# Hybrid backbone, one core: direct products in one block, Fourier products among value tiles, smaller angle tables given later

## The chip, the cores and the metric

The kernel runs on one core of one Trainium2 chip. The metric is the device time of one execution in microseconds (us), the median over runs. The core has a matrix engine (PE), a vector engine (DVE), an activation engine (ACT), a general engine (POOL), and SyncE (SP), whose instruction queue issues the DMA transfers spoken of here. Each engine works through its own list of instructions in order, and semaphores hold an instruction back until what it needs is there.

## What is computed

Two layers over 2048 latent tokens (a grid 64 wide) and 256 context tokens, 1024 channels. Layer 0 has a Fourier mixer (256 channels) beside a neighbourhood attention (12 heads of 64), layer 1 a gated MLP beside a bidirectional S5 scan. Cut to what matters here:

```python
def even_mixer(hl, hc, w_in, w_out, rpb, with_ctx_out):
    fa_l, ga_l, q_l, k_l, v_l, gb_l = split_cols(hl @ w_in, EVEN_SPLITS)
    ...
    a_l = fourier_mix(fa_l) * jax.nn.silu(ga_l)
    n_l = neighbourhood_attention(heads(q_l), heads(k_l), heads(v_l), k_c, v_c, rpb) * jax.nn.silu(gb_l)
    y_l = jnp.concatenate([a_l, n_l], axis=-1) @ w_out

def fourier_mix(v):
    y = jnp.fft.fftn(vg, axes=(1, 3), norm="ortho").real   # vg: (B, L, groups, 64)

def s5_direction(u_lat, u_ctx, lam_re, lam_im, log_step, b_re, b_im, c_re, c_im, reverse, with_ctx_out):
    lam_bar, b_bar = s5_discretise(lam_re, lam_im, log_step, b_re, b_im)
    ...
    h_lat = linear_scan(lam_bar, drive(u_lat), h_end, reverse)
    return read(h_lat), ...
```

The tables of the S5 scan depend on the weights alone: powers of `lam_bar` ("turn" tables), products of those with `B` and `C`, and a 16-step convolution kernel worked out from them ("direct products").

## The kernel before

All of what the change touches lies in the first fifth of the kernel, in `run()`. Weights in float32 are split into two float16 parts: the load fills a staging buffer `wf` (L154, a ring of four), DVE takes the maximum per partition (L156), PE and DVE take it across partitions (L109, L111) and to a power of two (L92 to L100), ACT writes the high part `wh` (L189) and DVE the low part `wl` (L190). A product is then three groups of eight matmuls of 256 or 512 columns (L181), and its result is split again in the same way (ACT L189, DVE L190).

`run()` calls, one after another: `s5_prep` (with `v_proj` of the first and second block of 256 value channels handed in as work to lie between), `v_proj(2)` for the third block, `fourier_first`, and `need((0, 5))`, which starts `heads`, the queries, keys and gates of the first pair of heads and the attention's first loads. The written order is not the order on the engines: each call gives its instructions in a stream ("", "b", "f") with PSUM banks of its own, and a scheduler then merges the streams by its own estimate of times, for each engine. Where a tile's memory is used again, the new owner waits for the old one.

- `v_proj(blk)`: 18 tiles of 128 tokens by 256 channels, each 24 matmuls on PE, one eviction on ACT, one on DVE, two stores.
- `s5_prep`: complex products (`cmul`, L1109 to L1114) on DVE and POOL, tables `W` written to DRAM (`mo_d`), then, after `v_proj(1)`, in pool "s5pk": eight groups `q` of direct products. Each loads a tile `ws` (576 KB, L1314) and a tile `bs` (64 KB, L1315) from DRAM, two buffers each, multiplies them in 32 small matmuls (L1319), copies four strips out on ACT (L1328), adds `db` on DVE (L1329) and stores `kp_d` (L1330).
- At the end of the same pool: eight angle tables. Each is a complex product of the two turn tables, six DVE instructions of 1152 columns (L1109 to L1114 by way of `cmul`), into a tile `rot` that is stored in `rot_d` (1152 KB). They are read again only in the S5 scan of layer 1 (`E`).
- `fourier_first`: 16 products of a table `d1` with a strip `Z` of the Fourier input, both loaded (L559, L561, three buffers each), 4 matmuls each on PE (L564), copied on ACT (L566) and stored (L567); then two context products (L573, L577).
- `heads` for pair 0 begins with three weight loads and splits, and then runs on PE (L181).

## Time and profile before

| what | us |
|---|---|
| median of three runs | 2430.7 (2428.79 to 2432.24) |
| the profiled execution, its own time | 2425.14 |
| its span (first to last instruction) | 2423.3 |
| PE busy in the span | 2219.7 |
| DVE busy | 1579.7 |
| ACT busy | 1050.9 |
| POOL busy | 336.3 |

One execution was profiled; the 1.8 us beside the span lie around the program. "Busy" leaves out register, branch and DMA-issuing instructions. In rows of a timeline the columns are start, duration, engine, line, operation, output and inputs with their shape, how many like it were merged, and in brackets the idle time ahead and who ended it. `PEclk` is the granted clock of PE as a share of full speed.

### The profile page before, as it was taken

To read this page: it belongs to the slowest core of one execution; us is meant where nothing else is said; L and a number is where in the kernel's file an instruction comes from. 1 tells how busy PE (TensorE), PEld (TensorE's weight loads), DVE (VectorE), ACT (ScalarE), POOL (GpSimd) and SP (SyncE) were. 2 spreads that over 40 slices of the span, in tenths; PEclk is the share of its full clock that TensorE was granted. 3 is DMA by queue.
4 is the path that set the end of the run, shared out by engine and by line. 5 is a ranking of instruction groups with operands and counts; after the bars stand their busy time and mean duration, and the time that the engine had idled before them with its cause. 6 is when DMAs were issued, how large, how long until landed. Compare 5 with 4: busy or idle time off the path is not lost. (4 is left out here: it accounts for less than half of the span.)

```text
span 2423.3 us, 42852 instructions
## 1 busy us (share of the span) xinstructions
PE 2219.7 (92%) x15860; PEld 1421.6 (59%) x15860; DVE 1579.7 (65%) x3949; ACT 1050.9 (43%) x2212; POOL 336.3 (14%) x457
## 2 busy tenths in 40 slices
PE   5999885999999999999978899997899999999998
PEld 2668773476665767666657466556555565444443
DVE  5888892266567666666569667774496952458455
ACT  4822222155555656565557454552221221334332
POOL 0102200022222322222234000000010011110000
PEclk8999998999999999999998899998899999999999
DMA  9844677413335243433342444545466751256332
GB/s 320 264 108 127 168 236 231 131 54 95 115 103 149 81 119 106 116 114 93 96 167 86 137 140 135 158 134 164 143 182 195 200 152 48 80 156 194 122 113 87
DMA packets 349971, 340.57 MB, mean 141 GB/s; under 512 B 94482, under 2 KB 291486, under 8 KB 347970
## 3 DMA queue, kind: packets, MB, share of 16 engines
q1 hardware_dynamic: 349650, 337.80, 46.5%
q8 instruction: 125, 2.05, 0.4%
q14 instruction: 84, 0.69, 0.1%
q10 hardware_dynamic: 112, 0.03, 0.0%
HBM read 218.43 MB, written 110.91 MB: 136 GB/s over the span
## 5 line engine op out<-in xcount | busy, mean ns | idle before, releaser
L181 PEld LDWEIGHTS <-wh 128*128 128x128 f16 x2944 | 281.8, 99 | 169.0 <-issue 9.2
L1000 DVE CUSTOM_DVE_ANT_0 P<-S,bias,slab 128x640 f32<-128x640 f32 (+2 forms) x216 | 193.6, 896 | 161.0 <-PE S L997 157.0
L189 ACT ACTIVATE ph<-PT 128x384 f16<-128x384 f32 (+1 forms) x408 | 172.6, 456 | 216.4 <-PE PT L1016 215.6
L181 PEld LDWEIGHTS <-wl 128*128 128x128 f16 x1472 | 144.0, 100 | 112.0 <-issue 27.4
L190 DVE SCALAR_TENSOR_TENSOR pl<-PT,ph 128x384 f16<-128x384 f32 (+1 forms) x408 | 195.0, 508 | 13.8 <-ACT ph L189 12.4
L949 POOL TENSOR_TENSOR bias<-G,masks 128x384 f32<-128x384 f32 (+1 forms) x144 | 152.3, 1058 | 345.5 <-DVE t L1000 322.5
L1002 ACT ACTIVATE P<-P,t 128x640 f32<-128x640 f32 (+2 forms) x216 | 181.2, 839 | 41.4 <-DVE t L1000 40.0
L181 PE MATMUL pg<-hh,wl 128*128 128x512 f16 (+1 forms) x800 | 184.6, 365 | 13.7 <-DVE stg L190 5.6
L181 PEld LDWEIGHTS <-h1p 128*128 128x128 f16 x1152 | 111.1, 98 | 136.6 <-issue 8.8
L181 PE MATMUL pu<-wh,h1p 128*128 128x512 f16 x768 | 179.9, 379 | 1.6 <-DMA h1p<-h 1.6
L181 PE MATMUL pg<-hl,wh 128*128 128x512 f16 (+1 forms) x800 | 181.2, 360 | 0.0
L181 PE MATMUL pg<-hh,wh 128*128 128x512 f16 (+1 forms) x800 | 181.2, 359 | 0.0
L181 PEld LDWEIGHTS <-yh 128*128 128x128 f16 x1088 | 106.8, 98 | 125.4 <-issue 2.7
L1016 PE MATMUL PT<-ident,P 128*128 128x128 f32 x1104 | 162.3, 277 | 11.3 <-DVE pl L190 9.8
L997 PEld LDWEIGHTS <-Q 128*128 128x128 f16 x1776 | 131.6, 98 | 63.1 <-issue 22.7
L997 PE MATMUL S<-K,Q 128*128 128x128 f16 (+1 forms) x1776 | 158.4, 233 | 2.4 <-DVE t L1000 2.2
L181 PE MATMUL pg<-wh,yl 128*128 128x512 f16 x544 | 133.3, 386 | 5.2 <-DVE yl L190 5.1
L1016 PEld LDWEIGHTS PT<-ident,P 128*128 128x128 f32 x1104 | 120.3, 142 | 20.2 <-issue 6.8
L181 PE MATMUL pg<-wl,yh 128*128 128x512 f16 x544 | 131.3, 382 | 0.0
L156 DVE TENSOR_REDUCE t<-wf 128x1 f32<-128x1024 f32 x68 | 82.4, 1216 | 74.8 <-DMA wf<-in_w_in_even_dram 27.0
L181 PE MATMUL pg<-wh,yh 128*128 128x512 f16 x544 | 130.3, 379 | 0.0
L181 PEld LDWEIGHTS <-hh 128*128 128x128 f16 x1152 | 115.5, 100 | 15.7
(344 smaller groups left out, 3952.6 us busy)
## 6 DMA issues: line engine op xcount, KB each, us to landing
wada<-in_w_ada_dram SPq DMA_DIRECT2D x34, 512.0 KB
x<-in_x_dram SPq DMA_DIRECT2D x32, 512.0 KB
wf<-in_w_in_even_dram SPq DMA_DIRECT2D x28, 512.0 KB
V<-vs SPq DMA_DIRECT2D x192, 64.0 KB
K<-kd SPq DMA_DIRECT2D x96, 128.0 KB
wf<-in_w_in_odd_dram SPq DMA_DIRECT2D x20, 512.0 KB
rot_d<-rot SPq DMA_DIRECT2D x8, 1152.0 KB
Y<-ys SPq DMA_DIRECT2D x144, 64.0 KB
```

Source lines behind the costliest of these rows:

```text
L156: nc.vector.tensor_reduce(m[:, i:i + 1], f, axis=AX.X, op=OP.max, apply_absolute_value=True)
L181: nc.tensor.matmul(ps, a(k), b(k), start=(n == 0), stop=(n == 3 * kb - 1))
L189: nc.scalar.activation(hi, src, AF.Copy, scale=scale)
L190: nc.vector.scalar_tensor_tensor(lo, src, scale, hi, op0=OP.mult, op1=OP.subtract)
L949: nc.gpsimd.tensor_tensor(q4(bv), gv, q4(masks[:, m0:m0 + 128 * nch]), op=OP.add)
L997: nc.tensor.matmul(S[:, at:at + m], u["q"], K[:, hl, off:off + m], start=(hl == 1), stop=(hl == 0))
L1000: nc.vector.tensor_tensor_reduce(P[:, 0:n], S[:, 0:n], u["B"][:, 0:n], u["negf"], 3.4e38, OP.add, OP.min, nm)
L1002: nc.scalar.activation(P[:, 0:n], P[:, 0:n], AF.Exp, bias=nm, scale=-1.0, accum_out=l)
L1016: self.nc.tensor.transpose(PT[:, c - a:c - a + 128], P[:, c:c + 128], self.ident)
```

## The change

`s5_prep` keeps only the tables up to `v_proj(1)`. The direct products move to a function `s5_direct`, and their tiles `ws` and `bs` are halved: 16 loads of 288 KB and 16 of 32 KB in place of 8 and 8, still two buffers each. The angle tables move to `s5_angles`: 16 tables in place of 8, six DVE instructions of 576 columns each, one of the two products made in place in the table (`tq` is the only other tile, one buffer); `rot_d` has a new layout and `s5_states` reads it contiguously. The turn tables and the angle tiles lie in pools of their own, on the right side of memory.

Ahead of `v_proj(2)`, `heads` is started and stepped until its first pair's weights are loaded and split. `fourier_first` becomes a generator: its first four pairs of loads are given ahead of `v_proj(2)`, its products after it in stream "f", with four buffers for `d1` and `Z` and two for the copies. The angle tables are given after that.

```diff
@@ run() @@
-                    with self.stream("b"):
-                        self.s5_prep([lambda: self.v_proj(gp, 0), lambda: self.v_proj(gp, 1)])
-                    self.v_proj(gp, 2)
-                    qp = hTs.enter_context(self.pool_("qkg"))
-                    with self.pool_("fft") as fp, self.stream("f"):
-                        self.fourier_first(fp)
-                    self.gpool = hTs.enter_context(self.pool_("gates"))
-                    self.steps = self.mixed(self.heads(qp), self.ada_steps(), ADA_EVERY)
-                    self.ahead, self.credit, self.at, self.made = None, 0.0, (0, 0), -1
-                    self.need((0, 5))
+                    with self.pool_("s5r", side="right") as rp, self.pool_("s5e", side="right") as ep:
+                        with self.stream("b"):
+                            self.s5_prep(rp, [lambda: self.v_proj(gp, 0), lambda: self.v_proj(gp, 1)])
+                            self.s5_direct()
+                        qp = hTs.enter_context(self.pool_("qkg"))
+                        self.steps = self.mixed(self.heads(qp), self.ada_steps(), ADA_EVERY)
+                        self.ahead, self.credit, self.at, self.made = None, 0.0, (0, 0), -1
+                        while self.ahead is None:
+                            self.step()
+                        with self.pool_("fft") as fp:
+                            first = self.fourier_first(fp)
+                            next(first)
+                            self.v_proj(gp, 2)
+                            with self.stream("f"):
+                                for _ in first:
+                                    pass
+                        self.s5_angles(ep)
+                        self.gpool = hTs.enter_context(self.pool_("gates"))
+                        self.need((0, 5))
@@ s5_direct(), was in s5_prep() @@
             for q in range(8):
-                ws = pool.tile([128, 4, 2, 144], F32, name=self.name("ws"), tag="ws", bufs=2)
-                bs = pool.tile([128, 4, 2, 16], F32, name=self.name("bs"), tag="bs", bufs=2)
...
+                    if j == 0:
+                        g = 4 * q + j4
+                        ws = pool.tile([128, 2, 2, 144], F32, name=self.name("ws"), tag="ws", bufs=2)
+                        bs = pool.tile([128, 2, 2, 16], F32, name=self.name("bs"), tag="bs", bufs=2)
@@ s5_angles() @@
+        for i in range(16):
...
+            for r, op in ((0, OP.subtract), (1, OP.add)):
+                t = pool.tile([128, 2, 18, 16], F32, name=self.name("tq"), tag="tq", bufs=1)
+                nc.vector.tensor_tensor(v(e[:, r]), x[0], y[r], op=OP.mult)
+                nc.vector.tensor_tensor(t, x[1], y[1 - r], op=OP.mult)
+                nc.vector.tensor_tensor(v(e[:, r]), v(e[:, r]), t, op=op)
+            nc.sync.dma_start(self.rot_d[j, h, d], e.rearrange("p r g n -> p (r g n)"))
```

What the scheduler makes of it is seen in the lists of the engines; the lines of the changed kernel are some 20 further down (L1319 becomes L1346, L564 becomes L583, L1329 becomes L1356).

PE, before, where the second group of direct products ends (`ws_3674`, the second of eight) and the first tile of `v_proj(2)` begins (`pg_3980`, weights `wh_3973`):

```order
L1319 MATMUL pg_3678<-ws_3674,bs_3675 16x16 x2
L1319 MATMUL pg_3678<-ws_3674,bs_3675 16x112 x2
L1319 MATMUL pg_3678<-ws_3674,bs_3675 16x16 x2
L1319 MATMUL pg_3678<-ws_3674,bs_3675 16x112 x2
L1319 MATMUL pg_3678<-ws_3674,bs_3675 16x16 x2
L181 LDWEIGHTS hl_79
L181 MATMUL pg_3980<-wh_3973,hl_79 128x256
L181 LDWEIGHTS hl_79
L181 MATMUL pg_3980<-wh_3973,hl_79 128x256
```

PE, after, the same place (`ws_3898` is the last half of the last group, `mx_4026` the maximum over the weights of `v_proj(2)`, `Z` a Fourier strip, `wh_4038` the weights of `v_proj(2)`):

```order
L1346 MATMUL pg_3885<-ws_3898,bs_3899 16x112 x2
L1346 MATMUL pg_3885<-ws_3898,bs_3899 16x16 x2
L109 MATMUL mx_4026<-ident,t_4024 128x128
L583 MATMUL pg_4585<-Z_4003,d_639_4001 128x256 x2
L583 MATMUL pg_4595<-Z_4007,d_641_4005 128x256 x2
L583 MATMUL pg_4605<-Z_4011,d_643_4009 128x256 x2
L583 MATMUL pg_4615<-Z_4015,d_645_4013 128x256 x2
L583 MATMUL pg_4625<-Z_4590,d_695_4588 128x256 x2
L181 LDWEIGHTS hl_79
L181 MATMUL pg_4045<-wh_4038,hl_79 128x256
L181 LDWEIGHTS hl_79
```

Before, groups three to eight follow between tiles of `v_proj(2)`, and the 16 Fourier products stand in a row behind its last tile. Now all eight groups stand in one block with nothing of another stream between them; behind it come the maximum, five Fourier products and then `v_proj(2)`, whose tiles have the other eleven Fourier products between them.

DVE, before, among the complex products of `s5_prep`, at the start of `v_proj(1)` (`wl_3974` is the low part of the weights of `v_proj(2)`):

```order
L1112 TENSOR_TENSOR p_2718<-p_1862,p_1865 128x4x128
L1113 TENSOR_TENSOR p_2719<-p_1862,p_1864 128x4x128
L190 SCALAR_TENSOR_TENSOR wl_3974<-wf_3953,slab_217,wh_3973 128x1024
L1114 TENSOR_TENSOR p_2823<-p_2718,p_2719 128x512
L190 SCALAR_TENSOR_TENSOR wl_3974<-wf_3956,slab_217,wh_3973 128x1024
L190 SCALAR_TENSOR_TENSOR v_3115<-pg_3090,v_3115 128x4x64
```

DVE, after, behind the last adds of the direct products (`wl_3944`, `wl_3964`, `wl_3980` are the low parts of the first pair's weights, `wl_4039` that of `v_proj(2)`'s):

```order
L190 SCALAR_TENSOR_TENSOR wl_3964<-wf_3928,slab_217,wh_3963 128x1024
L190 SCALAR_TENSOR_TENSOR wl_3980<-wf_3948,slab_217,wh_3979 128x1024
L1373 TENSOR_TENSOR tq_4910<-turn_1858,turn_1857 128x576
L156 TENSOR_REDUCE t_4017<-wf_4021 128x1
L1374 TENSOR_TENSOR rot_4905<-rot_4905,tq_4910 128x576
L161 TENSOR_REDUCE t_4024<-t_4017 128x1
L156 TENSOR_REDUCE t_5160<-wf_5161 128x1
L156 TENSOR_REDUCE t_5224<-wf_5225 128x1
L111 TENSOR_REDUCE t_4028<-mx_4026 128x1
...
L190 SCALAR_TENSOR_TENSOR wl_4039<-wf_4018,slab_217,wh_4038 128x1024
L190 SCALAR_TENSOR_TENSOR wl_4039<-wf_4021,slab_217,wh_4038 128x1024
```

The weights of `v_proj(2)` are made 190 places later than before, behind the three splits of the first pair's weights. Of the angle tables' 96 instructions 58 stand between the turn tables and the last eviction of `v_proj(1)`, beside the same complex products and evictions as before; before there were 5 there.

SP, after, the end of the direct products' loads (`kp_d` and `rot_d` are stores; `wf_4021` is the second half of the weights of `v_proj(2)`, `wf_5161` and `wf_5225` belong to the second pair of heads):

```order
L1344 DMA bs_3887<-bst_d 128x4x16
L1343 DMA ws_3898<-mo_d 128x4x144
L1344 DMA bs_3899<-bst_d 128x4x16
L1357 DMA kp_d<-p_3636 128x240
L1375 DMA rot_d<-rot_4885 128x1152
L1357 DMA kp_d<-p_3637 128x240
L1375 DMA rot_d<-rot_4895 128x1152
L154 DMA wf_4021<-in_w_in_even_dram 128x4x256
L154 DMA wf_5161<-in_w_in_even_dram 128x8x128
L154 DMA wf_5225<-in_w_in_even_dram 128x8x128
```

Before, both halves of the weights of `v_proj(2)` are loaded ahead of the first value tiles. Now the second half comes behind the last store of `kp_d`, and takes the staging buffer that the first of the three splits gives back.

## Rows read from the trace of the kernel before

**Rows 1.** The page: busy time, and the chain that ended last.

```profile
PE 2219.7 (92%) x15860; PEld 1421.6 (59%) x15860; DVE 1579.7 (65%) x3949; ACT 1050.9 (43%) x2212; POOL 336.3 (14%) x457
...
PE 16%; DVE 1%; DMA 1%; issue 0%; ACT 0%; SPq 0%; ACTq 0%; DVEq 0%
```

**Rows 2.** Busy time by stretch: start and end, length, engines, clock, DMA.

```profile
188.20:292.60 104.40, 91.64 (x774) 79.17 (x771) 87.91 (x116) 26.27 (x65) 33.76 (x24) 0.93 0.54 145
292.60:357.60 65.00, 62.55 (x689) 55.65 (x688) 58.60 (x88) 18.14 (x50) 0.00 (x0) 1.00 0.77 235
357.60:415.40 57.80, 26.57 (x91) 17.20 (x90) 14.37 (x48) 13.87 (x22) 0.62 (x2) 0.84 0.65 223
```

**Rows 3.** Timeline of PE, Fourier stage and the start of heads.

```profile
373.98 6.63 PE L564 MATMUL pg<-Z,d 128*128 128x256 f32 x16 [16.27 <-DMA Z<-fa_d]
...
402.09 1.10 PE L564 MATMUL pg<-Z,d 128*128 128x256 f32 x4 [0.22 <-DMA Z<-fa_d]
403.02 1.88 PE L573 MATMUL pg<-dctx,zc 128*128 128x512 f32 x4
...
415.39 1.89 PE L181 MATMUL pg<-hh,wl 128*128 128x256 f16 x8 [3.94 <-DVE slab L717]
...
447.94 3.36 PE L181 MATMUL pg<-hh,wl 128*128 128x512 f16 x8 [3.76 <-DVE stg L190]
```

**Rows 4.** Matmuls of 292.6 to 415.4 by line and shape.

```profile
L564 PE MATMUL pg<-Z,d 128*128 128x256 f32 x64 | 19.7, 449 | 25.7 <-DMA Z<-fa_d 25.0 <-ACT a L566 0.8
L181 PE MATMUL pg<-wh,hh 128*128 128x256 f16 x145 | 19.3, 273 | 0.0
```

**Rows 5.** Timeline of PE, first direct products.

```profile
293.41 1.83 PE L1319 MATMUL pg<-ws,bs 128*16 128x112 f32 x32 [0.71 <-DMA bs<-bst_d]
295.81 1.83 PE L1319 MATMUL pg<-ws,bs 128*16 128x112 f32 x32 [0.57 <-DMA bs<-bst_d]
```

**Rows 6.** Timeline of DVE, products of 576 columns back to back.

```profile
237.94 0.74 DVE L1279 TENSOR_TENSOR p<-p,p 128x576 f32<-128x576 f32 x1
238.61 0.74 DVE L1278 TENSOR_TENSOR p<-p,p 128x576 f32<-128x576 f32 x1
```

**Rows 7.** DVE by line and shape, 188.2 to 292.6.

```profile
L190 DVE SCALAR_TENSOR_TENSOR v<-pg,v 128x256 f16<-128x256 f32 x29 | 12.0, 418 | 14.0 <-ACT v L189 13.8
...
L190 DVE SCALAR_TENSOR_TENSOR wl<-wf,slab,wh 128x1024 f16<-128x1024 f32 x2 | 3.4, 1696 | 0.0
L156 DVE TENSOR_REDUCE t<-wf 128x1 f32<-128x1024 f32 x2 | 2.3, 1200 | 0.0
...
L1110 DVE TENSOR_TENSOR p<-turn,turn 128x1152 f32<-128x1152 f32 x1 | 1.4, 1352 | 0.0
```

**Rows 8.** DMA issues of SP, first groups of direct products.

```profile
291.13 1.58 SPq L1315 DMA_DIRECT2D bs<-bst_d  x1
...
299.21 0.38 SPq L1314 DMA_DIRECT2D ws<-mo_d  x1
299.63 0.95 SPq L1315 DMA_DIRECT2D bs<-bst_d  x1
```

**Rows 9.** DMA issues of SP, last Fourier strip.

```profile
399.79 0.39 SPq L561 DMA_DIRECT2D Z<-fa_d  x1
```

**Rows 10.** ACT by line and shape, copies of the direct products.

```profile
L1328 ACT ACTIVATE p<-pg 16x240 f32<-16x240 f32 x32 | 11.5, 361 | 0.7
```

**Rows 11.** DMA issue of SP, a weight load.

```profile
417.72 0.38 SPq L154 DMA_DIRECT2D wf<-in_w_in_even_dram  x1
```

**Rows 12.** Timeline of DVE, maxima over loaded weights.

```profile
424.78 1.22 DVE L156 TENSOR_REDUCE t<-wf 128x1 f32<-128x1024 f32 x1 [0.99 <-DMA wf<-in_w_in_even_dram]
...
446.07 1.22 DVE L156 TENSOR_REDUCE t<-wf 128x1 f32<-128x1024 f32 x1 [10.89 <-DMA wf<-in_w_in_even_dram]
```

**Rows 13.** Timeline of PE, matmuls behind an idle stretch.

```profile
269.55 1.03 PE L181 MATMUL pg<-wh,hl 128*128 128x256 f16 x8 [2.86 <-DVE v L190]
...
271.86 1.92 PE L181 MATMUL pg<-wh,hh 128*128 128x256 f16 x8
```

More of the change, by code (lines that the diff above doesn't have):

```diff
@@ L556, in fourier_first, with load @@
         self.gg_d = self.dram.tile([2, 128, SEQ], F32, name="gg_d")
+        got = []
+        def load():
+            n2 = len(got)
+            dt = pool.tile([128, 2, 128], F32, name=self.name("d1"), tag="d1", bufs=4)
+            nc.sync.dma_start(dt, I["k_dft1"][:, n2])
+            Z = pool.tile([128, 256], F32, name=self.name("Z"), tag="Z", bufs=4)
+            nc.sync.dma_start(Z, dap(self.fa_d, n2 * 256, [[16 * 256, 128], [1, 256]]))
+            got.append((dt, Z))
+        for _ in range(4):
+            load()
+        yield
         for n2 in range(16):
-            dt = pool.tile([128, 2, 128], F32, name=self.name("d1"), tag="d1", bufs=3)
-            nc.sync.dma_start(dt, I["k_dft1"][:, n2])
-            Z = pool.tile([128, 256], F32, name=self.name("Z"), tag="Z", bufs=3)
-            nc.sync.dma_start(Z, dap(self.fa_d, n2 * 256, [[16 * 256, 128], [1, 256]]))
+            dt, Z = got[n2]
             ps = self.psg()
@@ L564, in fourier_first @@
                 nc.tensor.matmul(ps[:, cs * 256:(cs + 1) * 256], dt[:, cs, :], Z, start=True, stop=True)
-            a = pool.tile([128, 512], F32, name=self.name("a1"), tag="a1", bufs=3)
+            if n2 < 12:
+                load()
+            a = pool.tile([128, 512], F32, name=self.name("a1"), tag="a1", bufs=2)
             nc.scalar.activation(a, ps, AF.Copy)
@@ L1123, in s5_prep @@
         bst_d = self.dram.tile([32 * 4 * 64, 16], F32, name="bst_d")
-        self.rot_d = self.dram.tile([4, 2, 128, 2 * 4 * 288], F32, name="rot_d")
+        self.rot_d = self.dram.tile([4, 2, 2, 128, 2 * 2 * 288], F32, name="rot_d")
         self.mag8 = self.const.tile([128, 32], F32, name="mag8")
-        rots = ExitStack()
-        rp = rots.enter_context(self.pool_("s5r"))
-        turn = [rp.tile([128, 2, 32, n], F32, name=f"turn{n}") for n in (16, 18)]
+        self.turn_t = turn = [rp.tile([128, 2, 32, n], F32, name=f"turn{n}") for n in (16, 18)]
         with self.pool_("s5p") as pool, ExitStack() as early:
@@ L1330, in s5_prep, with s5_angles @@
                 self.bq.dma_start(self.kp_d[q], kp)
[L1332 to L1341 removed]
+    def s5_angles(self, pool):
+        nc = self.nc
+        turn = self.turn_t
+        v = lambda a: a.rearrange("p g (b k) -> p g b k", k=16)
+        for i in range(16):
+            j, h, d = i // 4, i // 2 % 2, i % 2
+            e = pool.tile([128, 2, 2, 288], F32, name=self.name("rot"), tag="rot", bufs=2)
+            q = slice(16 * d + 2 * (i // 2), 16 * d + 2 * (i // 2) + 2)
+            x = [turn[1][:, r, q, :, None].to_broadcast([128, 2, 18, 16]) for r in range(2)]
+            y = [turn[0][:, r, q, None, :].to_broadcast([128, 2, 18, 16]) for r in range(2)]
+            for r, op in ((0, OP.subtract), (1, OP.add)):
[4 more added lines that the diff above has]
+            nc.sync.dma_start(self.rot_d[j, h, d], e.rearrange("p r g n -> p (r g n)"))
     def out_proj(self, pool, lh, ll, w, u_y, ssq, sx, sq=None):
```

28 lines of the change are left out of this document (11 added, 17 removed).

## The prediction

> **What bounds the kernel now.** The page comes first. PE is busy 2219.7 of 2423.3 us and DVE 1579.7, and the chain that ended last is PE's where it names an engine [rows 1]. So the kernel is bound by PE, and what can be gained is about 200 us in which PE stands idle. The table by stretch then shows where that is for this change [rows 2]. Up to 292.6 (end of `v_proj(1)`) PE works 91.64 of 104.40 us, and DVE 87.91: DVE is nearly full here. From 292.6 to 357.6 (direct products among the tiles of `v_proj(2)`) PE works 62.55 of 65.00. From 357.6 to 415.4, the Fourier stage, PE works 26.57 of 57.80 at a granted clock of 0.84: 31 us of idle time, and slow matmuls besides. These 31 us are what there is to win. The timeline tells why: the first Fourier product waits 16.27 us for its strip `Z`, the products take until 403 us, two context products follow, and after 3.94 us more (the split of the first pair's weights) `heads` starts at 415.39 [rows 3]. By line, the Fourier products waited 25.0 us for `Z` and worked 19.7 [rows 4].
>
> **The change: what I compare.** All parts end before the start of `heads`, so I work out that moment, 415.4 before, and correct for what comes later. On PE, 122.8 us lie between 292.6 and 415.4. The PE work in them is: direct products 8 x 1.83 = 14.6 [rows 5]; `v_proj(2)`, 18 tiles of 24 matmuls (145 of one of their three kinds [rows 4]), about 48, which is what the direct products leave of the 62.55 [rows 2]; 16 Fourier products, 0.93 each from start to start (402.09 to 403.02), 15; two context products of two parts, the longer part 1.88 each, 6 in all [rows 3]. Together 84; some 39 us are holes and half clock. The change can save no more than these 39 here.
>
> **Angle tables moved up: `v_proj(1)` ends later.** The order has 58 angle instructions ahead of the last eviction of `v_proj(1)`, 5 before. One of 576 columns takes 0.67 us from start to start (237.94 to 238.61) [rows 6], so 58 are 38.9 us on DVE. Out of the stretch go 5 of 1152 columns at 1.35, and the two splits (3.4) and two maxima (2.3) of weights [rows 7], 12.4 in all. DVE's work is then 87.9 - 12.4 + 38.9 = 114.4 us, where the stretch is 104.4 long [rows 2]: DVE alone makes it 10 us longer. Its idle time of 16.5 us was almost wholly waiting for ACT's half of an eviction, 14.0 [rows 7], which is PE not being ready; with DVE late most of that goes. I keep 3.5 us of it: +13.5, with bounds of +7 (some tables slip behind, evictions are drained by the three `v` buffers) and +20 (half of the idle time stays). Before, 43 angle instructions ran beside the well-fed PE of `v_proj(2)`, and hid there; that cover is given up.
>
> **Direct products in a block: their loads come into the open.** Before, six of the eight groups lay between tiles of `v_proj(2)`, 47 us of PE work that covered every load. Now PE has nothing else from the first to the last. The loads come through two buffers of half a group. When a half is done its buffers are free; SP issues two loads (0.38 and up to 0.95 [rows 8]), they land, and PE multiplies 0.92. The landing: the second group's issue ended at 292.71 and its products started at 295.81, 3.1 us [rows 5, 8]; the last strip `Z`, issued at 399.79, was used at 402.09, 2.3 us [rows 3, 9]; counted from the start of the issue of `bs` it was 4.7. With 3.1, two halves take 0.1 + 0.9 + 3.1 + 0.9 = 5.0, and eight such rounds, less the two halves that are there at the start, 36 to 38 us. SP also has some 20 other DMAs in its row there (stores of `kp_d` and `rot_d`, the first Fourier loads, 0.4 each), and the stores wait for DVE; I take 41 us for the whole block. From below: the fastest that SP can issue 32 loads and 24 others, at 0.38 to 0.45 each, is 24, and the 10 MB that move in the block (5 of loads, 4 of tables, 1 of the rest) at the 235 GB/s of [rows 2] take 42, at twice that rate 21. So 24 to 50 by these rows, and 20 in a case that stands among the rivals, against 14.6 of plain work.
>
> The Trainium skill, "DMA: Bandwidth & Descriptors", section "Anatomy of one DMA — SWDGE (gpsimd) path", gives each DMA of that path a fixed cost of about 2.0 us that no size takes away, plus bytes / 436 GB/s. These loads are SP's, so it is a neighbour and no more; an estimate by it is 2.7 us for a half tile `ws` and 3.4 for a whole one: halving the tile saves a fifth of the landing and doubles their number, which speaks against this part of the change. By 2.7 the block would be 38 us and not 41.
>
> **The weights of `v_proj(2)` come last.** Before, they were split at the start of `v_proj(1)`, and nothing waited. Now their second half is behind the last store of `kp_d` in SP's list, and needs a staging buffer that only the first pair's first split frees. That split writes into memory which the direct products' pool held, so it waits for the last `kp_d` to land. From the last direct product to the first matmul of `v_proj(2)`: four copies of 0.36 [rows 10] and an add 1.7, store landing 3.1 as above, the split's two parts 2.8 (low part 1.7 at most [rows 7], high part as an estimate 1.1), the load of 512 KB (issued at 417.72, used at 424.78 [rows 11, 12]) 7.1, its maximum 1.2, the two other maxima that stand ahead in DVE's list 2.4 [rows 7], and from the maximum across partitions to split weights 3.9, as the first pair's took before [rows 3]: 22 us, bounds 18 (the load in 3.1) and 25. PE has five Fourier products in this time (about 7 us at the slow clock: four of them took 6.63 [rows 3]), which cost nothing. The clock falls behind such holes: after 2.86 us of waiting eight matmuls soon took 1.92 us where they had taken 1.03 [rows 13]; a few such groups at the start of `v_proj(2)`, 2 to 3 us, are inside the bounds.
>
> **What is won.** Behind it PE has `v_proj(2)` 48, eleven Fourier products at 0.93, 10.2, and context products 6: 64.2, and I take 64.5; the loads of `Z` are hidden by the tiles (four buffers, and two tiles of 2.6 us between products). The 31 us of idle time in the Fourier stage are gone, and so is the split of the first pair's weights (3.94 of it). `heads` starts at once.
>
> **The sum.** 292.6 + 13.5 + 41 + 22 + 64.5 = 433.6, or 18.2 us later than 415.4. After that, the order of all engines is as before but for the second pair's weights, which are now loaded early. Their maximum on DVE waited 10.89 us and held up an eviction, and PE stood 3.76 us and then ran eight matmuls in 3.36 instead of 1.89 [rows 3, 12]. That goes, 5.5 with the slow matmuls after it; what would be late next is the fourth weight load, which I leave at nothing, with a bound of 2 us. The new reading of the tables in layer 1 costs nothing: it is the same bytes, loaded ahead. So 18.2 - 5.5 = +12.7 us on the profiled execution's 2425.1: 2437.8. The median of the runs is 5.6 above that execution, so 2443 us as a median.
>
> **Rivals.**
> - *The loads keep up.* While PE works on one half the other lands: if SP issues at once and a half lands within some 1.3 us of that, the block is PE's 14.6 us and 16 waits of about 0.35, 20 us. The sum is then 21 less, `heads` starts at 412.6, and with the later 5.5 the kernel is 8.3 us faster: 2422. For it: the two waits that the trace shows for whole groups were 0.71 and 0.57 only [rows 5]. Against it: these were the first two groups, loaded into empty buffers, and every landing in the trace took 2.3 us or more. It decides below 23 us for the block.
> - *The pieces cancel.* A block of 34 us, angle tables at +9, 20 of chain: 419.6, 4.2 late, with the later gain 1 early: 2430.
> - *DVE is the wall.* If the idle time stays in `v_proj(1)` (+20), and the adds of the direct products stand behind 38 more angle instructions (25 us on DVE, in the same block) so that stores, copies and loads wait in turn and the block takes 50: 292.6 + 20 + 50 + 23 + 64.5 = 450, with the later gain 29 late: 2460. For it: DVE is at 84% before anything is added. Against it: in the block DVE has 25 us of work in 41.
> - *The change doesn't do what it says,* that is, the Fourier products don't fill anything: the order shows eleven of them between the tiles, so I give it nothing of its own; it would show as PE waiting for `Z` among the tiles.
>
> **How the numbers follow.** Forecast (+5 to +23 us) 0.50; loads keep up 0.14; pieces cancel 0.17; DVE is the wall 0.19. The time is that of the forecast, 2443. The range reaches from the lower side of "the pieces cancel", 2427, to 2460, and leaves out "loads keep up" and the worst of the last. About 0.2% is what a measurement of this kernel can tell from no change, 4.9 us: slower 0.69, within 0.17, faster 0.14.
>
> **What would show it right or wrong.** Right: `v_proj(1)` ends near 306; PE waits for `ws` or `bs` in most of the 16 halves and the block is about 40 long; some 20 us with only Fourier products; then tiles with no wait for `Z`; `heads` starts near 433 and there is no 3.8 us hole after its tenth eviction or so. Wrong: DVE idle in `v_proj(1)`, or products of one half straight behind the other, or the weights of `v_proj(2)` ready when the block ends (then 20 us of the sum are gone, and it is faster). The chain of 22 is the longest piece with no row of its own; if it is half, the result is even.

## The result: 0.5% slower, `heads` start 22.7 us late

The changed kernel takes 2439.23 us (median of 10 runs, 2435.32 to 2441.26) and the kernel before 2426.72 (10 runs on the same chip, 2420.06 to 2432.24): a ratio of 1.0051, 95% interval 1.0039 to 1.0062. That is 12.5 us slower; forecast were 12.7. The profiled execution of the changed kernel has a span of 2438.7 us, 15.4 more than that of before.

The page of the kernel after says little: PE (2218.4 us) and DVE (1582.6 us) are as busy as before, and the chain that ended last is PE's again [rows 1].

The table by stretch of the kernel after answers [rows 2]; I have put the borders where its own stages end: `v_proj(1)`, the block of direct products, the chain to the first tile of `v_proj(2)`, the tiles, and the start of `heads` (438.1). The columns are start and end, length, busy time of PE, PE's weight loads, DVE, ACT and POOL with counts, granted clock, DMA share, GB/s.

```profile
188.20:305.50 117.30, 93.96 (x793) 80.24 (x790) 115.19 (x166) 25.54 (x64) 35.51 (x24) 0.94 0.52 153
305.50:356.70 51.20, 25.71 (x257) 21.06 (x256) 28.55 (x66) 10.55 (x30) 0.00 (x0) 0.61 0.83 227
356.70:376.20 19.50, 7.29 (x22) 6.01 (x23) 16.45 (x29) 7.82 (x12) 0.00 (x0) 0.63 0.65 217
376.20:438.10 61.90, 61.14 (x489) 52.12 (x488) 11.70 (x23) 15.50 (x34) 0.00 (x0) 1.00 0.51 161
```

DVE is busy 115.2 of the first 117.3 us, and PE is busy 94.0 of them. In the second stretch PE is busy half the time at a granted clock of 0.61, and in the third, 19.5 us long, little more than a third. In the fourth PE is busy 61.1 of 61.9 at the full clock: there the change does what it is for. The timeline of PE, which answers [rows 3, 5]:

```profile
304.47 1.04 PE L181 MATMUL pg<-wh,hh 128*128 128x256 f16 x8
312.39 3.54 PE L1346 MATMUL pg<-ws,bs 128*16 128x112 f32 x32 [6.88 <-DMA bs<-bst_d]
...
336.26 3.16 PE L1346 MATMUL pg<-ws,bs 128*16 128x112 f32 x32 [2.44 <-DMA bs<-bst_d]
342.72 3.19 PE L1346 MATMUL pg<-ws,bs 128*16 128x112 f32 x32 [3.30 <-DMA bs<-bst_d]
348.00 3.27 PE L1346 MATMUL pg<-ws,bs 128*16 128x112 f32 x32 [2.09 <-DMA bs<-bst_d]
353.24 3.39 PE L1346 MATMUL pg<-ws,bs 128*16 128x112 f32 x32 [1.97 <-DMA bs<-bst_d]
368.91 0.79 PE L109 MATMUL mx<-ident,t 128*128 128x128 f32 x2 [12.28 <-DVE t L161]
369.50 6.89 PE L583 MATMUL pg<-Z,d 128*128 128x256 f32 x20
376.23 1.91 PE L181 MATMUL pg<-wh,hl 128*128 128x256 f16 x16
...
438.13 1.04 PE L181 MATMUL pg<-hh,wl 128*128 128x256 f16 x8
```

The last group of `v_proj(1)` starts at 304.47, the first direct product at 312.39, 6.88 us after PE fell idle. A row of 32 is two halves straight behind each other. The last of these pairs follow each other at 5.2 to 6.5 us (336.26, 342.72, 348.00, 353.24), and PE waits for `bs` ahead of each pair. From the end of the last product (356.63) PE waits 12.28 us for the maximum of the weights of `v_proj(2)`, does five Fourier products, starts `v_proj(2)` at 376.23 and `heads` at 438.13. The hole of 3.76 us that stood behind the 18th group of `heads` [rows 3] is gone.

The links of the chain stand in the timelines of ACT, DVE and SP, one row or two of each:

```profile
360.32 3.23 ACT L189 ACTIVATE wh<-wf,slab 128x1024 f16<-128x1024 f32 x3 [2.13 <-DMA kp_d<-p]
```

```profile
361.99 1.28 DVE L190 SCALAR_TENSOR_TENSOR wl<-wf,slab,wh 128x1024 f16<-128x1024 f32 x1
...
366.92 1.21 DVE L156 TENSOR_REDUCE t<-wf 128x1 f32<-128x1024 f32 x1
```

```profile
166.66 9.81 SPq L154 DMA_DIRECT2D wf<-in_w_in_even_dram  x4
...
306.26 0.89 SPq L1343 DMA_DIRECT2D ws<-mo_d  x1
...
363.30 3.43 SPq L154 DMA_DIRECT2D wf<-in_w_in_even_dram  x3
```

All four staging buffers were filled between 166.66 and 176.47, with the three loads of the first pair's weights and the first half of those for `v_proj(2)`, and no other load of weights is issued until 363.30. The high part of the first pair's weights (L189, 360.32) waits for the landing of `kp_d`, the low part follows at 361.99, and only when it has freed its staging buffer does SP issue the load of the second half for `v_proj(2)` (363.30, the first of three); its maximum is taken at 366.92.

### The profile page after: what moved, and what is told of

It reads as the page before. It is cut to its first block, busy times and chain, and to the rows that moved or that the text cites. A ratio compares the mean times of both kernels' runs of the same rounds, so it can differ in the third digit from the quotient of the medians.

```text
span 2438.7 us, 42935 instructions
## 1 busy us (share of the span) xinstructions
PE 2218.4 (91%) x15860; PEld 1424.2 (58%) x15860; DVE 1582.6 (65%) x3997; ACT 1051.6 (43%) x2212; POOL 337.4 (14%) x457
## 5 line engine op out<-in xcount | busy, mean ns | idle before, releaser
L189 ACT ACTIVATE ph<-PT 128x384 f16<-128x384 f32 (+1 forms) x408 | 172.5, 457 | 217.0 <-PE PT L1037 215.8
L190 DVE SCALAR_TENSOR_TENSOR pl<-PT,ph 128x384 f16<-128x384 f32 (+1 forms) x408 | 194.9, 508 | 14.0 <-ACT ph L189 12.6
```

The costliest lines, as they stand in the source:

```text
L189: nc.scalar.activation(hi, src, AF.Copy, scale=scale)
L190: nc.vector.scalar_tensor_tensor(lo, src, scale, hi, op0=OP.mult, op1=OP.subtract)
```

## The experiments

Two theories stood against each other. **Mine:** three debits (angle tables on DVE in `v_proj(1)`, a block of direct products that waits for its loads, the weights of `v_proj(2)` at the end of a chain) against one credit (Fourier products among the tiles). **The rivals:** the loads keep up, the pieces cancel, DVE is the wall, or the Fourier products fill nothing; for the block of direct products, also that bytes or SP's issues limit it and not round trips. The table sums up what was measured. "First value tile" is the start of `v_proj(0)` on PE, ahead of all the work that the edits move. It differs by up to 5 us between the profiled executions, the profiles don't show why, and moments further right carry that difference: the changed kernel is 1.5 us late there already. "First logits" is the start of the attention's first product on PE (470.35 in the kernel before); behind it all kernels have nearly the same work ahead of them. Ratios are against the kernel before, run beside each.

| kernel | ratio (95%) | first value tile | `v_proj(1)` ends | last direct product starts | first logits |
|---|---|---|---|---|---|
| before | 1 | 167.2 | 292.6 | among tiles | 470.4 |
| after | 1.0051 (1.0039 to 1.0062) | 168.7 | 305.5 | 353.2 (of a pair) | 485.9 |
| whole tiles | 1.0025 (1.0013 to 1.0037) | 166.8 | 305.3 | 343.0 (of two pairs) | 481.9 |
| four buffers | 0.9992 (0.9976 to 1.0008) | 170.2 | 306.8 | 339.4 | 473.9 |
| late angle tables | 1.0016 (1.0000 to 1.0031) | 168.4 | 301.6 | 336.6 | 472.9 |
| a third of the tables' work | 0.9996 (0.9980 to 1.0012) | 168.8 | 299.2 | 343.0 | 472.0 |
| own memory for the pair's weights | 0.9973 (0.9962 to 0.9984) | 167.1 | 304.2 | 356.5, among tiles | 457.7 |
| first pair last | 0.9931 (0.9908 to 0.9954) | 168.0 | 308.0 | among tiles | 456.4 |
| first pair last, late tables | 0.9912 (0.9896 to 0.9927) | 170.2 | not told apart | among tiles | 452.3 |
| `v_proj(2)`'s weights first | 0.9863 (0.9839 to 0.9887) | 168.5 | not told apart | among tiles | 444.1 |
| the same, whole tiles | 0.9888 (0.9871 to 0.9906) | 169.4 | not told apart | among tiles | 447.9 |
| the same, late tables | 0.9866 (0.9849 to 0.9883) | 168.4 | not told apart | among tiles | 442.9 |
| Fourier alone | 0.9973 (0.9961 to 0.9984) | 171.8 | not told apart | among tiles | 471.0 |

**Is the block bound by round trips? (whole tiles, four buffers).** The first kernel undoes the halving of `ws` and `bs` in the changed kernel, with two buffers of whole groups:

```diff
-                        ws = pool.tile([128, 2, 2, 144], F32, name=self.name("ws"), tag="ws", bufs=2)
-                        bs = pool.tile([128, 2, 2, 16], F32, name=self.name("bs"), tag="bs", bufs=2)
+                ws = pool.tile([128, 4, 2, 144], F32, name=self.name("ws"), tag="ws", bufs=2)
+                bs = pool.tile([128, 4, 2, 16], F32, name=self.name("bs"), tag="bs", bufs=2)
```

> The changed kernel with the halving of ws and bs undone: 8 + 8 loads of whole groups, two buffers. The block of direct products took 51 us in the changed kernel (305.5 to 356.7). Theory A, the block is bound by round trips (free buffer, issue, landing): one buffer now holds 1.85 us of products and two groups need one round trip of about 7.5 us (issue 1.3, landing 4, products 1.9), four rounds and a start of 7: 37 us, so 10 to 14 us less than the changed kernel, about 2427. Theory B, it is bound by the bytes that move beside it (tables, strips, loads, 227 GB/s): the same bytes, the same 51 us, 2439. Theory C, SP's issue is the limit: 16 issues fewer at 0.45, 7 us less, 2432.

The second leaves the halves and gives them four buffers (`bufs=4` on both lines).

> The changed kernel with four buffers for the halves of ws and bs in place of two, same loads. Theory A (round trips): four halves share one, some 6.5 us with 3.7 us of products at the full clock, 16 halves in about 26 us and a start of 7: 33 us in place of 51, about 2422. Theory B (bytes): 51 us stay, 2439. Theory C (SP's issue): 51 us stay, 2439, since as many issues are made.

Measured: 1.0025 and 0.9992. The timelines of PE, whole tiles first, then four buffers; the row of the maximum (L109) belongs to the chain behind the block:

```profile
334.35 5.83 PE L1343 MATMUL pg<-ws,bs 128*16 128x112 f32 x64 [4.24 <-DMA bs<-bst_d]
343.01 4.99 PE L1343 MATMUL pg<-ws,bs 128*16 128x112 f32 x64 [2.83 <-DMA bs<-bst_d]
362.07 0.79 PE L109 MATMUL mx<-ident,t 128*128 128x128 f32 x2 [14.08 <-DVE t L161]
```

```profile
336.17 2.91 PE L1346 MATMUL pg<-ws,bs 128*16 128x112 f32 x32 [0.54 <-DMA bs<-bst_d]
339.42 1.03 PE L1346 MATMUL pg<-ws,bs 128*16 128x112 f32 x16 [0.34 <-DMA bs<-bst_d]
354.82 0.79 PE L109 MATMUL mx<-ident,t 128*128 128x128 f32 x2 [14.37 <-DVE t L161]
```

The block is 42.7 us long with whole tiles (305.3 to 348.0) and 33.6 with four buffers (306.8 to 340.4), where it was 51.2. With the same bytes in both, theory B falls. Theory C had 7 us less for whole tiles, and the time (6 us less by the ratios) fits that better than A's 10 to 14; but four buffers, with the same count of issues as the changed kernel, took 17.6 us off the block, where C had nothing. What counts is how many products stand behind one round trip. A's 37 us for whole tiles were 6 too few, its 33 for four buffers were right. The chain to the first tile of `v_proj(2)` stays, 21.1 and 22.0 us here (19.6 from the end of the last product in the changed kernel). So halving the tiles at two buffers cost 8.5 us here, and four buffers of halves, which take as much memory as two whole tiles, are 9 us better than those, in the length of the block.

**What does DVE cost? (late tables, a third of the work).** The third kernel holds back the tables' stores; with two buffers for tables, the tables behind them wait too:

```diff
-                        self.s5_angles(ep)
+                        with self.tc.issue_after(self.v_mid.ins):
+                            self.s5_angles(ep)
```

> The changed kernel with the stores of the angle tables held back until the first tile of v_proj(2) is stored; with two table buffers only some 15 of the 96 angle instructions then lie ahead of the end of v_proj(1), in place of 58. Theory A, DVE is what lengthened v_proj(1): it ends near 293 again, 12 us earlier, and the tables run on DVE beside v_proj(2), where it has room (16 of 62 us were used): about 2427. Rival: the 12 us come back because the tables now stand between the adds of the direct products or the splits of the weights: 2435 to 2440.

The other one leaves the tables where they are and does two of their six instructions:

```diff
                 nc.vector.tensor_tensor(v(e[:, r]), x[0], y[r], op=OP.mult)
-                nc.vector.tensor_tensor(t, x[1], y[1 - r], op=OP.mult)
-                nc.vector.tensor_tensor(v(e[:, r]), v(e[:, r]), t, op=op)
```

> The changed kernel with four of each angle table's six instructions left out (the second product and the sum, so the tables hold one product only); stores and everything else stay. DVE then has 21 us of tables in all. Theory A, DVE's load lengthened v_proj(1) by 12.8 us and nothing else of the change is DVE's doing: it ends near 293, block and chain stay at 51 and 19.5, and the time is 12 us less than the changed kernel, 2427, or 1.000 of the kernel before. Rival 1, the tables on DVE also stretch the block: 18 to 20 us less, 0.997. Rival 2, v_proj(1) is late for another reason: 1.005.

Measured: 1.0016 and 0.9996, that is 8 and 13 us less than the changed kernel where A had 12 for both. The total is about A's, the place is not. `v_proj(1)` ends at 301.6 and 299.2, not at 293. (The 16 us that the expectation of the late tables gives as DVE's work beside `v_proj(2)` are ACT's 15.50; DVE's are 11.70.) The timeline of PE with a third of the work, end of `v_proj(1)` and start of the block:

```profile
298.14 1.04 PE L181 MATMUL pg<-wh,hh 128*128 128x256 f16 x8
302.61 3.13 PE L1346 MATMUL pg<-ws,bs 128*16 128x112 f32 x32 [3.43 <-DMA bs<-bst_d]
```

Here the wait ahead of the first direct product is 3.43 us and not 6.88, and the stretch from the end of `v_proj(1)` to the end of the last product 45.6 us and not 51.2. So the work that was left out had cost about 6 us in `v_proj(1)` and 6 in the block: rival 1's place, A's price. The table by stretch of that run, `v_proj(1)` and block (columns as above):

```profile
188.20:299.20 111.00, 93.91 (x794) 80.65 (x791) 100.38 (x145) 25.28 (x64) 34.04 (x24) 0.94 0.66 207
299.20:344.80 45.60, 26.12 (x256) 21.33 (x256) 6.03 (x31) 10.52 (x30) 0.00 (x0) 0.64 0.74 182
```

DVE has 14.8 us less to do in `v_proj(1)` than in the changed kernel (100.4 and not 115.2), but only 6.3 us of it come back as time; the other 8.5 turn into idle time of DVE, 10.6 us of the 111.0 where the changed kernel has 2.1. That is the idle time which I had thought would go, and it means that PE and DVE wait for each other in turn here.

With late tables 24 matmuls of direct products (about 2 us) lie ahead of the end of `v_proj(1)`, so its 301.6 is no clean measure of the tables.

What still keeps `v_proj(1)` from ending at 292.6 in both runs can be read where the first tables run. The table by stretch, 192 to 207 us, of the kernel before, the changed kernel, late tables and a third of the work, and two rows of DVE in the changed kernel:

```profile
192.00:207.00 15.00, 13.70 (x126) 12.21 (x124) 13.47 (x18) 3.50 (x14) 6.77 (x5) 1.00 0.34 83
192.00:207.00 15.00, 8.57 (x63) 6.74 (x61) 15.00 (x20) 2.26 (x8) 6.26 (x4) 0.77 0.14 36
192.00:207.00 15.00, 8.57 (x62) 6.64 (x61) 15.00 (x20) 2.01 (x9) 6.26 (x4) 0.77 0.14 34
192.00:207.00 15.00, 10.29 (x74) 8.10 (x72) 14.16 (x20) 3.15 (x13) 6.27 (x4) 0.77 0.32 107
```

```profile
191.32 3.84 DVE L1372 TENSOR_TENSOR rot<-turn,turn 128x576 f32<-128x576 f32 x4 [0.78 <-ACT turn L1222]
...
198.10 1.81 DVE L1373 TENSOR_TENSOR tq<-turn,turn 128x576 f32<-128x576 f32 x1
```

PE did 126 matmuls in these 15 us before, and 63, 62 and 74 in the three others: at 0.109 us each it falls 5.7 to 7 us behind here. The products of the first tables stand on DVE ahead of two evictions, and PE waits for those (5.26, 5.66 and 3.86 us; the wait in the kernel before is 1.30) and then runs at a lower clock. Neither run took these products away: two table buffers let the first tables through, and a third of the work leaves four products. So nearly all of what `v_proj(1)` loses is the tables' after all, about half of it at the first two; this half is read from the rows, no run tested it.

**Where does the chain come from? (own memory).** One pool is opened earlier, and nothing else is changed, so that the first pair's weights no longer take over what the direct products held:

```diff
                         with self.stream("b"):
                             self.s5_prep(rp, [lambda: self.v_proj(gp, 0), lambda: self.v_proj(gp, 1)])
+                        qp = hTs.enter_context(self.pool_("qkg"))
+                        with self.stream("b"):
                             self.s5_direct()
-                        qp = hTs.enter_context(self.pool_("qkg"))
```

> The changed kernel with one pool opened earlier: the memory of the first pair's weights and queries ('qkg') no longer takes over what the direct products' pool held. Nothing else differs. Theory A, the chain of 19.5 us and the empty block come from this reuse: the first split waits for the last kp_d store, the staging buffer is freed only then, so the weights of v_proj(2) can't be made. With own memory the list of PE has v_proj(2) tiles from the middle of the direct products on: half of the block stays (25 us), the chain is gone, heads start near 405 in place of 438: 2408 to 2416 where the kernel before takes 2427. Rival, the order of the loads on SP decides and not the memory: the chain stays, 2439.

Measured: 0.9973, 7.8 per mille below the changed kernel. Timelines of ACT, SP and PE:

```profile
301.90 3.21 ACT L189 ACTIVATE wh<-wf,slab 128x1024 f16<-128x1024 f32 x3
```

```profile
308.34 1.12 SPq L154 DMA_DIRECT2D wf<-in_w_in_even_dram  x1
```

```profile
334.21 3.29 PE L181 MATMUL pg<-wh,hl 128*128 128x256 f16 x16 [2.78 <-ACT wh L189]
...
356.46 1.85 PE L1347 MATMUL pg<-ws,bs 128*16 128x112 f32 x32
```

The split of the first pair's weights is done from 301.90 on and not from 360.32, with no wait for `kp_d`, and the second half of the weights of `v_proj(2)` is loaded from 308.34 on and not from 363.30. The tiles of `v_proj(2)` start at 334.21, 42 us earlier than in the changed kernel, with four groups of direct products still to come, which now lie among tiles with no wait of over 0.3 us. Heads start at 399.64. So the reuse of memory, with the ring of four staging buffers, made both the chain and the second half of the block. The rival (SP's order) falls: the weight loads stand in the same order among themselves, and it was the memory that let them move up. The size was off: heads start 5 us earlier than A had, the first logits are 28 us earlier, and by the ratios the time is only 19 us less, where A had 23 to 31. The profiled execution (2417.51) was 6.8 us under the median of this kernel, so profile and median don't agree well here, and the difference stays open.

**What is the credit worth? (order of the weights).** The next kernel puts the first pair's weights behind `v_proj(2)`, where they were in the kernel before; the weights of `v_proj(2)` are then ready early:

```diff
-                        self.steps = self.mixed(self.heads(qp), self.ada_steps(), ADA_EVERY)
-                        self.ahead, self.credit, self.at, self.made = None, 0.0, (0, 0), -1
-                        while self.ahead is None:
-                            self.step()
...
                         self.gpool = hTs.enter_context(self.pool_("gates"))
+                        self.steps = self.mixed(self.heads(qp), self.ada_steps(), ADA_EVERY)
+                        self.ahead, self.credit, self.at, self.made = None, 0.0, (0, 0), -1
                         self.need((0, 5))
```

> The changed kernel without the early start of heads: the first pair's weights come after v_proj(2) as before, so the weights of v_proj(2) are ready early and its tiles lie among the direct products and the Fourier products. The angle tables stay early. Theory A, what costs is the order of the weights, which empties PE for the block and the chain behind it (51 + 19.5 us with 33 us of work): v_proj(1) ends at 305 as in the changed kernel, then 48 + 14.6 + 15 + 6 = 84 us of filled PE, then 5 us for the first pair's split: heads start near 395 in place of 438, of which some 7 go again later for the second pair's weights: about 2405. Rival: the loads of ws, bs and Z stay behind the tiles too, as two buffers of halves cover half as much, and the order gives back no more than 20: 2420.

Measured: 2406.92 us, 0.9931. Heads start at 400.81 (395 expected, 438.1 in the changed kernel), behind a wait of 3.95 us for their split, and the hole behind their 18th group is back:

```profile
400.81 1.89 PE L181 MATMUL pg<-hh,wl 128*128 128x256 f16 x8 [3.95 <-DVE slab L736]
...
433.50 3.57 PE L181 MATMUL pg<-hh,wl 128*128 128x512 f16 x8 [5.08 <-DVE stg L190]
```

The kernel after that gives both early, but those of `v_proj(2)` first:

```diff
+                        w2 = self.v_weights(gp, 2)
                         qp = hTs.enter_context(self.pool_("qkg"))
...
-                            self.v_proj(gp, 2)
+                            self.v_proj(gp, 2, w2)
```

(`v_weights` is the load and split that stood in `v_proj`.)

> The changed kernel with one thing moved: the weights of v_proj(2) are loaded and split ahead of the first pair's weights, and both ahead of v_proj(2). The angle tables stay early. Theory A, what cost 51 + 19.5 us is that v_proj(2) had no weights while the direct products waited for loads: v_proj(1) ends at 306, then 84 us of filled PE, heads start near 391 without a wait for their split, and the hole that the second pair's weights leave (5.1 us and slow matmuls in the run with the first pair last) is gone too: about 2392. Rival: the staging buffers and the memory that the first pair's weights wait for hold up the tiles or the start of heads: 2405.

Measured: 2400.49 us, 0.9863 (0.9839 to 0.9887), A's number (2392 is 0.986 of the kernel before). Against the changed kernel the move is worth some 45 us by the ratios, and 42 at the first logits. One wait of 2.57 us for the first group's loads is left of the block, heads start at 386.25 without waiting, among the last Fourier products, which wait once for `Z`:

```profile
318.24 3.20 PE L1349 MATMUL pg<-ws,bs 128*16 128x112 f32 x32 [2.57 <-DMA bs<-bst_d]
...
386.25 0.27 PE L181 MATMUL pg<-hh,wl 128*128 128x256 f16 x1
388.30 1.10 PE L586 MATMUL pg<-Z,d 128*128 128x256 f32 x4 [1.78 <-DMA Z<-fa_d]
```

With whole tiles in this kernel:

> The run with the weights of v_proj(2) ahead (0.986 of the kernel before), with ws and bs in whole groups. Theory A, halving costs only where PE has nothing else to do; under the tiles both are hidden: 0.986 again, within 4 us of that run. Rival, halving costs SP and the queues something everywhere: 5 to 8 us faster than that run, 0.983.

Measured: 0.9888 (0.9871 to 0.9906), 6 us more than the halves by the ratios, but the intervals overlap: under the tiles of `v_proj(2)` the halving costs nothing that shows. The rival's 5 to 8 us are not there; if anything the whole tiles are slower.

**Tables and weights together.** Late tables were put into both kernels:

> The run before with the first pair's weights after v_proj(2) (2407), and the stores of the angle tables held back until the first tile of v_proj(2) is stored as well. Theory A, the tables' price lies in v_proj(1) and DVE has room beside v_proj(2): v_proj(1) ends at 293 in place of 307, heads start near 388 in place of 401, and the time is 12 us less, 2395. Rival: the tables now delay the evictions and the splits beside v_proj(2) and the time stays: 2405.

> Both: the weights of v_proj(2) ahead of the first pair's, and the stores of the angle tables held back until the first tile of v_proj(2) is stored. Theory A, the two debits add up: v_proj(1) ends at 293, heads start near 379, 2380. Rival: DVE beside v_proj(2) is full (38 + 25 us of tables, 8 of evictions, 10 of splits in 62 us), so the two don't add: 2388 to 2392.

Measured: 0.9912 and 0.9866. With the first pair last, late tables bring some 5 us by the ratios, whose intervals overlap, and the first logits are 4 us earlier; A had 12. The split of the first pair now comes later still, since DVE has the tables, and PE waits 8.26 us for it instead of 3.95. With the weights of `v_proj(2)` first they bring nothing; the rival holds there. The price of the tables is not a fixed one: moved away from `v_proj(1)` they meet the next thing that needs DVE.

```profile
400.93 1.89 PE L181 MATMUL pg<-hh,wl 128*128 128x256 f16 x8 [8.26 <-DVE wl L190]
```

**The Fourier stage alone.** The kernel before with the generator, the four buffers and the loads ahead:

```diff
-                    self.v_proj(gp, 2)
                     qp = hTs.enter_context(self.pool_("qkg"))
-                    with self.pool_("fft") as fp, self.stream("f"):
-                        self.fourier_first(fp)
+                    with self.pool_("fft") as fp:
+                        first = self.fourier_first(fp)
+                        next(first)
+                        self.v_proj(gp, 2)
+                        with self.stream("f"):
+                            for _ in first:
+                                pass
```

> The kernel before with only the Fourier products given as in the change (first loads ahead of v_proj(2), products in a stream of their own behind its start), the angle tables left in the pool of the direct products. In the engines' lists the 16 products stay in a row behind the last tile of v_proj(2). Theory A, the Fourier tiles get their memory only when the angle tables have left it, so the products can't move and the time is that of the kernel before, 2425. Rival: the four buffers and the earlier loads alone shorten the Fourier stage (16.3 us of first wait, 8.7 of others): 2410.

Measured: 0.9973 (0.9961 to 0.9984). Timelines of PE and SP:

```profile
378.23 2.05 PE L578 MATMUL pg<-Z,d 128*128 128x256 f32 x4 [16.37 <-DMA Z<-fa_d]
```

```profile
370.48 0.32 SPq L1356 DMA_DIRECT2D rot_d<-rot  x1
...
373.58 0.45 SPq L568 DMA_DIRECT2D Z<-fa_d  x1
```

The first product still waits 16.37 us and stands behind the last tile, and the first load of `Z` is issued 3 us behind the store of the last angle table: theory A's mechanism. The ratio is 0.3% under 1, though, some 6 us. The moments in the profile (first logits 471.0, span 2424.3 us) are no earlier than before, but this execution was 4.6 us late at the first value tile already. Counted from there the first logits are 3.9 us earlier. Of these, 2.1 us are the Fourier stage, which takes 39.3 us from the first product to the start of `heads` (417.53) and not 41.4: the rival has a small part of its 15. The remaining 2 or 3 us stay open. Other runs fit the reading that angle tables in memory of their own let the Fourier products move (there the products lie among the tiles, also with late tables), but no run changed that memory alone.

## Why the prediction was right, and where it was not

It was right in sign and size (12.5 us measured, 12.7 forecast), and its three debits and its credit are there. That the two numbers agree to 0.2 us is luck. The block was 10.2 us longer than forecast, and the other four terms together 7.4 us shorter. That leaves the 15.4 us of the profiled pair, 1.5 of which lie ahead of the first value tile; the medians happen to differ by 3 us less. The time itself was forecast as 2443 us and is 2439.23, since ten runs of the kernel before have a median 4 us under that of the first three. Step by step:

| term | forecast | measured |
|---|---|---|
| end of `v_proj(1)` | 292.6 + 13.5 | 292.6 + 12.9 |
| block of direct products | 41 | 51.2 |
| chain to the first tile | 22 | 19.5 |
| tiles to the start of `heads` | 64.5 | 61.9 |
| start of `heads` | +18.2 | +22.7 |
| later | -5.5 | -7.2 (first logits +15.5) |
| sum, profiled pair | +12.7 | +15.4 (span) |

- *Angle tables.* The sum of DVE's work, 114.4 us, was measured as 115.2. It came out for a reason that I hadn't, so this too is luck in part: the price of 0.67 us is that of an instruction with POOL at rest. Rows of DVE by shape, kernel after, 188.2 to 305.5:

```profile
L1373 DVE TENSOR_TENSOR tq<-turn,turn 128x576 f32<-128x576 f32 x19 | 19.7, 1036 | 0.0
L1372 DVE TENSOR_TENSOR rot<-turn,turn 128x576 f32<-128x576 f32 x19 | 16.0, 882 | 1.9 <-DMA rot_d<-rot 1.1 <-ACT turn L1222 0.8
...
L1132 DVE TENSOR_TENSOR p<-p,p 128x512 f32<-128x512 f32 x4 | 2.7, 674 | 0.0
```

The tables' instructions took 0.88 and 1.04 us on the mean, while most of the complex products came down to 0.67. In the kernel before, the slow ones were these, as a row of the same view (188.2 to 292.6) shows:

```profile
L1113 DVE TENSOR_TENSOR p<-p,p 128x512 f32<-128x512 f32 x4 | 6.5, 1628 | 0.0
```

In both kernels POOL works some 34 to 36 us of the stretch, and what DVE does meanwhile is stretched (the last section shows it). The total is the same, the owner of the loss is another. Of the 12.9 us, 1.5 lie ahead of the first value tile, the run with a third of the tables' work took 6.3 away, and most of the rest falls at the first two tables; the other half of that run's gain is in the block.
- *The block.* The term was 10 us too small. I had the round trip nearly right (5.0 against 5.5 us for two halves) but deducted two halves "that are there at the start". They were not: SP issued the first `ws` at 306.26, after the end of `v_proj(1)`, behind stores of `mo_d` and `rot_d` that DVE's late work held up, and its issue and landing are the wait of 6.88 us. In the kernel before it was issued at 286.91, and with a third of the tables' work at 296.75, both ahead of the end of `v_proj(1)`. Within the round trip two errors made up for each other: the products ran at a mean granted clock of 0.61, about 1.6 us a half and not 0.92, and the landing was shorter, some 2.6 us from the end of the issue of `bs` ahead of the pairs at 348.00 and 353.24 and not 3.1. PE waited ahead of ten of the 16 halves, nine times for loads; the other six followed straight behind the first of their pair, which I had listed as a sign of being wrong, though one round trip for two halves is what the sum itself goes by. That two buffers and round trips set it, and not bytes or issues, the two runs on buffers showed: two whole groups took 8.7 us (334.35 to 343.01), two groups in halves 11. The Trainium skill, "DMA: Bandwidth & Descriptors", section "Anatomy of one DMA — SWDGE (gpsimd) path", has a fixed cost for each DMA that size doesn't take away; for these loads of SP the trace agrees in direction: a round of two halves took 5.5 us, and one of two whole groups, with twice the bytes, 8.7.
- *The chain.* Right in its links, each of which stands in the rows of the result; 2.5 us shorter, mostly as the load took 3.6 us from issue to use (363.30 to 366.92) and not 7.1, and two other maxima behind it then waited for their loads. The run with own memory shows the cause.
- *What was won.* The tiles with the Fourier products took 2.6 us less than forecast: PE stood idle for 0.8 us of them in all and ran at the full clock, and one context product of 0.9 us comes behind the start of `heads`.
- *Later.* The hole of 3.76 us went, as forecast; with the matmuls at the full clock behind it, it was 7.2 us in all and not 5.5.
- *The rivals.* "Loads keep up" needed a block of 20 us; it was 51. "The pieces cancel" needed 34, and `v_proj(1)` at +9; they were 51.2 and +12.9 (its own sum is 420.1, not 419.6). "DVE is the wall" had the block right (50) and `v_proj(1)` wrong (+20); of its mechanism a part holds, since the block came down from 51.2 to 45.6 with two thirds of the tables' work gone. "The change doesn't do what it says" falls: PE never waited for `Z` among the tiles. That 20 us of the sum would be gone if the weights were ready when the block ends, which stood there as what would make it wrong, is what the run with the weights of `v_proj(2)` first shows, and it was worth more than that, 45 us, since the block is then filled as well.

## What to carry to other kernels

Work that is given early on one engine takes its buffers and its memory early too: before moving weights forward, look up who waits for the staging buffers and the memory that they hold; here the order of two weight loads was worth some 45 us, where the whole change cost 12.5. Here loads that were hidden under long matmuls could be cut small at no cost that showed; the same loads in the open, through two buffers, cost a round trip for each pair, and more buffers of the same total size were worth more than larger tiles. Work that is to fill a hole pays only if it is ready when the hole comes: the eleven Fourier products, 10 us, and the value tiles came behind the block and the chain, in which PE stood idle for 38 us.

## What the runs showed of the hardware

- DVE's products of two tensors in SBUF took more than twice as long while POOL did the same kind of work. Timelines of DVE and of POOL, kernel after:

```profile
212.93 0.74 DVE L1299 TENSOR_TENSOR W<-p,p 128x576 f32<-128x576 f32 x1
...
213.93 1.61 DVE L1373 TENSOR_TENSOR tq<-turn,turn 128x576 f32<-128x576 f32 x1
215.46 1.65 DVE L1296 TENSOR_TENSOR W<-p,p 128x576 f32<-128x576 f32 x1
217.04 0.41 DVE L190 SCALAR_TENSOR_TENSOR v<-pg,v 128x256 f16<-128x256 f32 x1
```

```profile
213.82 1.11 POOL L1130 TENSOR_TENSOR p<-p,p 128x512 f32<-128x512 f32 x1 [14.52 <-DVE W L1299]
...
216.58 1.66 POOL L1132 TENSOR_TENSOR p<-p,p 128x512 f32<-128x512 f32 x1
```

POOL begins at 213.82. The instruction of 576 columns ahead of it took 0.74 us, the ones that start behind it 1.61 and 1.65, and the eviction between them (L190, 0.41 us as ever) isn't touched. From 188.2 to 305.5 us it is the same throughout: 102 such instructions of 512 or 576 columns that no product of POOL overlaps took 0.67 to 0.76 us, and 22 of the 26 that one overlaps took 1.32 to 1.83 (the other four fall on the start of a series on POOL). So, as an estimate from these rows, in the 1.6 us of one POOL product DVE gets through work of 0.67 and loses 0.9, where the same product on DVE would have taken 0.6 (from start to start); no run without POOL's part tested this.
- Matmuls with 16-column weights in a stretch with waits of 1 to 3 us between groups ran at a mean granted clock of 0.61, and at 1.00 among full tiles (3.2 us a group and not 1.85): here the waits for loads cost PE its clock besides the wait.
- The kernel before had medians of 2424.89, 2429.28 and 2430.71 us on three chips; the ratios against runs beside them are what can be compared.
